# Head 15 of a differential-attention layer as a row-scale batch of its own, with four token blocks' output products taken into the attention and partial sums kept in DRAM

## The chip, the cores and the metric

The kernel runs on one core of a Trainium2 chip. The metric is the device time of one execution in microseconds (us). The engines are named as in the profile: PE (TensorE matmul), PEld (its weight loads), DVE (VectorE), ACT (ScalarE), POOL (GpSimd), SP (SyncE, which issues most of the DMAs; ACT issues the rest). A "q" behind an engine's name, as in ACTq, is its instruction queue.

## The reference

Two decoder layers on a 1024 x 1024 input, cut here to what the change touches (layer 1, differential attention):

```python
h = rmsnorm(x, pre_norm_g[1])
q, k, v, g = split(h @ w_in)              # 16 heads, two query/key maps of 64 each, v of 128
probs = softmax(logits + rel_bias)        # causal
attn = probs[:, :, 0] - lam * probs[:, :, 1]
out = attn @ v
out = rmsnorm(out, subln_g) * (1 - lambda_init)   # per token and head: the "row scale"
gated = silu(g) * out
x = x + rmsnorm(gated @ w_out, post_norm_g[1])
```

The row scale of a head is only known when the head's values are done. It multiplies the gated values before the output projection, so the products of a head's columns with w_out have to wait for it.

## The kernel before

Every fp32 product is three matmuls on a high and a low part of both operands: high times high, high times low, low times high (`out_mm`, L122 to L124). The high part is made by a cast on ACT, the low part by a subtraction on DVE or POOL (L92/L94 for the output weights, where even slots go to DVE and odd ones to POOL; L110/L111 for the gated values of eight 128x128 tiles; L476/L477 for those of four).

Layer 1 runs 16 heads of 8 query blocks in the order 6, 2, 3, 7, 4, 0, 1, 5. For each block there are logits (L760, L767), a softmax (DVE and ACT, L792 to L803), transposes of the probabilities into one PSUM bank (`attn_t`, L821, then a cast `ath` at L824 on ACT and a subtraction `atl` at L825 on DVE) and, for each pair of blocks, the products with v (`values`, L835 to L837). Behind a pair come the square (L843), its split (`sqh` L844, `sql` L845), `go` (L851) and `square_sum` (L857, L858), whose row `ssr` goes to DRAM as `ssd` (L860, L861).

`row_scales` (L863 to L876) makes the scales of a batch of heads: ACT issues the DMA `rss<-ssd` (L867), PE transposes the softmax sums into the same single bank that `attn_t` uses (L869), DVE copies them (L872) and works out a reciprocal root, and ACT issues `rsd<-rsr` (L876), from which the scales are read back, broadcast. Batches before are heads 0 to 7, 8 to 11 and 12 to 15. The first two are scaled inside the attention on POOL (`finish`). The gates of heads from LATE = 12 on are not multiplied in the attention: they go to DRAM (`sgd`, L642), and the output stage reads raw values, gates and scales for each token block and multiplies them (`gated`, L464 to L471).

The order of PE is written by the code. Between the steps of the attention a generator (`filler_gen`) puts projections of later heads, then the gates of heads 12 to 15, then the first output products (kt 0 to 11 of token blocks 0 and 1, where a kt is one 128-row slice of w_out and 16 of them make a sum). How much is pulled in after each step is set by `fill_total` from planned totals (`total`, `late`, RATE). The orders of DVE, ACT, POOL and, before, SP come from the scheduler.

The output stage (`output_stage`) does the first 512 output columns for all eight blocks, then the other 512. `first` takes the sum of a finished block's first half: a Square on ACT (L508) and a product on DVE (L509). In layer 1 the banks of PSUM for it are six, taken in rotation, beside the two of the filler. Each engine works through its queue in order, so one waiting instruction holds all that stand behind it.

## Time and profile before

| | |
|---|---|
| time, three runs (us) | 2181.16, 2179.63, 2179.52 |
| median (us) | 2179.63 |
| the profiled execution's own time (us) | 2180.56 |
| its span, first to last instruction (us) | 2178.6 |
| PE busy (us) | 2130.3 |
| DVE / ACT / POOL busy (us) | 1293.9 / 851.5 / 427.4 |
| mean granted TensorE clock | 0.994 |

The span is what the trace covers; the time has 1.96 us more around it. The profiled execution is 0.93 us above the median. A busy engine is one that executes an instruction; issuing a DMA doesn't count.

### The profile page before, as it was taken

Reading aid. Unit: us, or ns where it says so; the run is one execution under the profiler, and the core shown is the slowest. Engines: PE = TensorE matmul, PEld = TensorE weight load, DVE = VectorE, ACT = ScalarE, POOL = GpSimd, SP = SyncE. Lnnn points to the kernel's source line nnn. Section 1 sums busy time; section 2 is a strip of 40 time slices with the busy share of each in tenths; the row PEclk is TensorE's granted clock in tenths of the full one; section 3 lists DMA queues with packets and bytes.
Section 4 is the critical chain, followed back from the end, with each engine's and each line's share of the span. In section 5 each row is a group of like instructions: output and inputs, shape, how many; then the busy total and the mean of one; then the engine's idle time right before and its main releaser. Section 6 shows DMA issues by size and latency. Waiting matters only on the chain.

```text
span 2178.6 us, 31078 instructions
## 1 busy us (share of the span) xinstructions
PE 2130.3 (98%) x11861; PEld 1793.9 (82%) x11861; DVE 1293.9 (59%) x3188; ACT 851.5 (39%) x1638; POOL 427.4 (20%) x246
## 2 busy tenths in 40 slices
PE   7999999999999999999999999999999999999998
PEld 7888988898897788787888888888787878877876
DVE  6254344434437438736777667777777777776644
ACT  4121221122123333335555455554545555544321
POOL 2332501511512000121111111111133111211300
PEclk9999999999999999999999999999999999999999
DMA  4112112111212544311111111111244113334743
GB/s 164 65 39 68 57 39 73 47 54 54 63 55 98 176 158 166 121 49 42 40 46 42 40 49 42 39 37 43 85 136 134 47 38 95 115 101 146 256 152 133
DMA packets 98916, 185.48 MB, mean 85 GB/s; under 512 B 8848, under 2 KB 51024, under 8 KB 98640
## 3 DMA queue, kind: packets, MB, share of 16 engines
q1 hardware_dynamic: 63824, 166.50, 23.5%
q10 hardware_dynamic: 34944, 17.01, 2.6%
q8 instruction: 93, 1.52, 0.3%
q14 instruction: 55, 0.45, 0.1%
HBM read 147.67 MB, written 38.95 MB: 86 GB/s over the span
## 4 chain that ended last, share of the span: by engine, by line
PE 89%; DVE 4%; DMA 3%; issue 2%; ACT 1%; SPq 0%; POOL 0%; DVEq 0%; ACTq 0%; POOLq 0%
PE ps_mm L158 6%; PE ps_mm L157 6%; PE ps_mm L159 5%; PE ps_mm L215 5%; PE ps_mm L216 5%; PE ps_mm L217 5%; PE ps_mm L122 4%; PE ps_mm L123 4%; PE ps_mm L124 4%; PE ps_t L821 3%; PE ps_ret L398 3%; PE ps_s L760 3%; PE ps_mm L658 3%; PE ps_mm L167 3%; PE ps_mm L169 3%; PE ps_mm L168 3%
## 5 line engine op out<-in xcount | busy, mean ns | idle before, releaser
L83 POOL TENSOR_TENSOR w_l<-w_raw,w_h 128x1024 fp32r<-128x1024 f32 x112 | 271.6, 2431 | 1169.3 <-ACT w_h L82 1137.6
L797 ACT ACTIVATE e<-ps_s,nm 128x896 f32<-128x896 f32 (+7 forms) x256 | 189.8, 742 | 111.3 <-DVE nm L795 101.9
L215 PE MATMUL ps_mm<-RB,w_h 128*128 128x512 f32 x512 | 209.8, 410 | 0.4 <-ACT RB L150 0.4
L157 PE MATMUL ps_mm<-RA,w_h 128*128 128x512 f32 x512 | 204.6, 400 | 1.2 <-DVE sg L428 1.1
L158 PE MATMUL ps_mm<-RA,w_h 128*128 128x512 f32 x512 | 205.4, 401 | 0.0
L216 PE MATMUL ps_mm<-RB,w_h 128*128 128x512 f32 x512 | 202.9, 396 | 1.5 <-DVE RB L151 1.5
L217 PE MATMUL ps_mm<-RB,w_l 128*128 128x512 f32 x512 | 202.7, 396 | 0.0
L159 PE MATMUL ps_mm<-RA,w_l 128*128 128x512 f32 x512 | 202.4, 396 | 0.0
L824 ACT CAST ath<-ps_t 128x512 fp32r<-128x512 f32 (+1 forms) x192 | 91.9, 478 | 221.4 <-PE ps_t L821 205.5
L82 ACT CAST w_h<-w_raw 128x1024 fp32r<-128x1024 f32 x112 | 117.5, 1049 | 123.5 <-PE ps_mm L158 38.8
L792 DVE TENSOR_REDUCE mx<-ps_s 128x1 f32<-128x640 f32 (+2 forms) x192 | 119.4, 622 | 76.7 <-PE ps_s L767 72.5
L111 DVE TENSOR_TENSOR g_l<-w_raw,g_h 128x1024 fp32r<-128x1024 f32 x60 | 84.1, 1402 | 107.4 <-ACT g_h L110 107.3
L658 PE MATMUL ps_mm<-w_h,RB 128*128 128x256 f32 x512 | 147.3, 288 | 0.0
L169 PE MATMUL ps_mm<-w_h,RA 128*128 128x256 f32 x512 | 145.6, 285 | 0.0
L167 PE MATMUL ps_mm<-w_h,RA 128*128 128x256 f32 x512 | 144.9, 285 | 0.6 <-ACT RA L150 0.6
L168 PE MATMUL ps_mm<-w_l,RA 128*128 128x256 f32 x512 | 144.8, 284 | 0.1
L660 PE MATMUL ps_mm<-w_h,RB 128*128 128x256 f32 x512 | 143.5, 280 | 0.0
L659 PE MATMUL ps_mm<-w_l,RB 128*128 128x256 f32 x512 | 143.5, 280 | 0.0
L110 ACT CAST g_h<-w_raw 128x1024 fp32r<-128x1024 f32 x60 | 62.9, 1049 | 167.9 <-PE ps_mm L123 125.5
L157 PEld LDWEIGHTS ps_mm<-RA,w_h 128*128 128x128 f32 x512 | 96.4, 188 | 24.7 <-DVE sg L428 1.6
L217 PEld LDWEIGHTS ps_mm<-RB,w_l 128*128 128x128 f32 x512 | 96.5, 189 | 23.7
L159 PEld LDWEIGHTS ps_mm<-RA,w_l 128*128 128x128 f32 x512 | 96.6, 189 | 22.4
(216 smaller groups left out, 5408.4 us busy)
## 6 DMA issues: line engine op xcount, KB each, us to landing
w_raw<-in_wn SPq DMA_DIRECT2D x64, 512.0 KB
w_raw<-in_wv SPq DMA_DIRECT2D x32, 512.0 KB
w_raw<-in_wo SPq DMA_DIRECT2D x32, 512.0 KB
w_raw<-g SPq DMA_DIRECT2D x32, 512.0 KB
w_raw<-g1f SPq DMA_DIRECT2D x24, 512.0 KB
xt<-in_x SPq DMA_DIRECT2D x16, 512.0 KB
w_raw<-in_wg SPq DMA_DIRECT2D x16, 512.0 KB
g<-go ACTq DMA_DIRECT2D x32, 256.0 KB
```

The lines of the kernel that those rows point to most:

```text
L83: nc.gpsimd.tensor_sub(l, raw, _f32(h))
L157: nc.tensor.matmul(ps, wh[:, k], region[:, kt, cols], start=(kt == 0), stop=False)
L158: nc.tensor.matmul(ps, wh[:, k], region[:, 8 + kt, cols], start=False, stop=False)
L159: nc.tensor.matmul(ps, wl[:, k], region[:, kt, cols], start=False, stop=(kt == KT - 1))
L167: nc.tensor.matmul(ps, region[:, kt, cols], wh[:, k], start=(kt == 0), stop=False)
L168: nc.tensor.matmul(ps, region[:, kt, cols], wl[:, k], start=False, stop=False)
L169: nc.tensor.matmul(ps, region[:, 8 + kt, cols], wh[:, k], start=False, stop=(kt == KT - 1))
L215: nc.tensor.matmul(ps, wh[:, k], HR[:, kt, tok], start=(kt == 0), stop=False)
L216: nc.tensor.matmul(ps, wh[:, k], HR[:, 8 + kt, tok], start=False, stop=False)
L217: nc.tensor.matmul(ps, wl[:, k], HR[:, kt, tok], start=False, stop=(kt == KT - 1))
L658: nc.tensor.matmul(ps[:, t, :], HR[:, kt, cols], wh[:, k], start=(kt == 0), stop=False)
L797: nc.scalar.activation(e[:, 0:n], S[:, 0:n], AF.Exp, bias=nm, accum_out=(s0 if m == 0 else s1))
```

## The change

LATE goes from 12 to 15, so that the gates of heads 12 to 14 are made before their values and multiplied into `go`. The batches become 0 to 7, 8 to 11, 12 to 14 and 15. `row_scales` now comes ahead of `attn_t` in the code. The filler computes kt 0 to 11 for four token blocks instead of two: the sums of blocks 0 and 1 are copied by ACT and sent to DRAM (`part`), those of blocks 2 and 3 stay in PSUM. The filler's output products wait for the first weights of w_out (`wo_loaded`). The output stage's part for layer 1 is the new `last_heads`, in which SP's order is that of the code: products of blocks 4 to 7; then pairs of blocks, whose heads 12 to 14 are scaled on POOL, stored, split and multiplied (kt 12 to 14); then head 15 for all eight blocks in one 128x1024 tile (kt 15), after which DVE adds the partial sums to blocks 0 and 1. The first `gated8` of the second half is loaded ahead (`ahead`).

```diff
-LATE = 12
+LATE = 15
+AHEAD_TB = 4
-BATCHES = ((0, 8), (8, 12), (12, 16))
+BATCHES = ((0, 8), (8, 12), (12, 15), (15, 16))
...
+        def load_pair(t0):
+            raw = fp.tile([P, 2, 3, P], F32, tag="praw", name="praw", bufs=2)
+            rb = fp.tile([P, 2, 3, P], F32, tag="prb", name="prb")
+            for t in range(2):
+                nc.sync.dma_start(raw[:, t], self.g1r[2][t0 + t])
+            for t in range(2):
+                nc.sync.dma_start(rb[:, t], self.rsd[2][t0 + t:t0 + t + 1].broadcast_to([P, 3, P]))
+            nc.gpsimd.tensor_mul(raw, raw, rb)
+            return raw
+
+        def store_pair(t0, raw):
+            for t in range(2):
+                nc.sync.dma_start(self.gsrc(1, t0 + t, 12, 3), raw[:, t])
+
+        def split_pair(raw):
...
+            nc.scalar.copy(gh, raw)
+            low = nc.vector.tensor_sub(gl, raw, _f32(gh))
+            return (gh, gl), low
...
+        with self.tc.manual_schedule(engines={SP}):
+            for t in range(6, 8):
+                self.load_out(1, slots, 0, t)
...
+            for tb in range(AHEAD_TB, TB, 2):
+                two = (tb, tb + 1)
+                gs[tb] = ([self.gated8(1, ((t, 0, 8),)) for t in two], self.gated8(1, tuple((t, 8, 4) for t in two)))
+                head += early(tb, *gs[tb])
+                raws[tb - AHEAD_TB] = load_pair(tb - AHEAD_TB)
...
+                second_half(tb - AHEAD_TB)
+            accs = [bank() for tb in range(AHEAD_TB - 2)] + head
+            rb = None
+            for t0 in range(0, TB, 2):
+                store_pair(t0, raws[t0])
+                g, low = split_pair(raws[t0])
+                if t0 + 4 < TB:
+                    raws[t0 + 4] = load_pair(t0 + 4)
...
+                if t0 >= 2 and t0 + 2 < TB:
+                    second_half(TB - AHEAD_TB + t0 - 2)
+                for t in range(2):
+                    tb = t0 + t
+                    for _ in self.out_mm(accs[tb], g, slots[0], 12, 3, 3 * t, k_first=12 if tb < AHEAD_TB - 2 else 0):
+                        pass
+            with self.tc.issue_after(low.ins):
+                nc.vector.tensor_mul(raw, raw, rb)
+            gh = self.wp.tile([P, TB, P], F32R, tag="wh", name="g_h", bufs=3)
+            gl = self.wp.tile([P, TB, P], F32R, tag="wl", name="g_l", bufs=3)
+            nc.scalar.copy(gh, raw)
+            with self.tc.issue_after(low.ins):
+                nc.vector.tensor_sub(gl, raw, _f32(gh))
+            ahead = self.gated8(1, ((0, 0, 8),))
+            nc.sync.dma_start(self.g1f[1][:, :, 7, :].rearrange("t p q -> p t q"), raw)
+            for tb in range(TB):
+                for _ in self.out_mm(accs[tb], (gh, gl), slots[0], 15, 1, tb):
+                    pass
+                first(tb, accs[tb], parts[:, tb, :] if tb < AHEAD_TB - 2 else None)
+        return ahead
...
+                while not wo_loaded:
+                    yield None
...
+                            part = wk.tile([P, 512], F32, tag="sg", name="part", bufs=3)
+                            nc.scalar.copy(part, pss[t])
+                            nc.scalar.dma_start(self.part[t0 + t], part)
...
-            late = (DH - LATE) * 10.4 + 15.6
+            late = (DH - LATE) * 10.4 + 7.8 * AHEAD_TB
...
+                if rows is not None:
+                    row_scales(*rows)
                 fill_until(ready)
                 attn_t(h, i, A, 0)
                 t_done = clk["pe"]
                 if rows is not None:
-                    row_scales(*rows)
...
-                    if i == ORDER[-1] and h + 1 in (BATCHES[0][1], BATCHES[1][1]):
+                    if i == ORDER[-1] and h + 1 in (BATCHES[0][1], BATCHES[1][1], BATCHES[2][1]):
```

Below, an order's row is an instruction's line, operation, and names out<-in; rows of the changed kernel carry its own line numbers. The number behind a name (`ssd_89`) tells versions of one name apart.

PE where the scales of heads 8 to 11 are made, at the start of head 12, before (ident,e are the transposes of the probabilities, ident,s0all that of the softmax sums):

```order
L858 MATMUL ps_o<-sql,ones 128x256
L760 MATMUL ps_s<-RA 128x384 x2
L767 MATMUL ps_s<-RA 128x384 x2
L821 MATMUL ps_t<-ident,e 128x128 x4
L869 MATMUL ps_t<-ident,s0all 32x128
L658 MATMUL ps_mm<-w_h,RB 128x256
```

and in the changed kernel:

```order
L939 MATMUL ps_o<-sql,ones 128x256
L841 MATMUL ps_s<-RA 128x384 x2
L848 MATMUL ps_s<-RA 128x384 x2
L950 MATMUL ps_t<-ident,s0all 32x128
L902 MATMUL ps_t<-ident,e 128x128 x4
L725 MATMUL ps_mm<-w_h,RB 128x256
```

The transpose of the sums has moved ahead of the four of the probabilities; the rest of the place is as it was.

DVE at the border of heads 14 and 15 in the changed kernel, where the scales of heads 12 to 14 are now made (L95 is the subtraction for a slot of w_out, L926 `sql`, L941 `ssr`, L906 `atl`, L953 and on the scales):

```order
L95 TENSOR_TENSOR RA<-w_raw,RA 128x1024
L930 SCALAR_TENSOR_TENSOR go<-ps_o,subg,sg 128x256
L926 TENSOR_TENSOR sql<-sq,sqh 128x256
L941 COPY ssr<-ps_o 1x256
L873 TENSOR_REDUCE mx<-ps_s 128x1
L953 COPY rsr<-ps_t 24x128
...
L95 TENSOR_TENSOR RA<-w_raw,RA 128x1024
L876 TENSOR_SCALAR nm<-mx 128x1
L906 TENSOR_TENSOR atl<-ps_t,ath 128x4x128
L955 SCALAR_TENSOR_TENSOR rsv<-rss,rsv 24x128
L66 TENSOR_SCALAR rsr<-rsv 24x128
```

ACT at the same place in the changed kernel (L93 is the cast for a slot of w_out, L925 `sqh`, L905 `ath`, L878 the exponentials):

```order
L924 ACTIVATE sq<-ps_o 128x256
L93 CAST RA<-w_raw 128x1024
L925 CAST sqh<-sq 128x256
L937 DMA g1r_80<-go 128x2x128
L942 DMA ssd_89<-ssr 2x1x128
L93 CAST RA<-w_raw 128x1024
L878 ACTIVATE e,s0all<-ps_s,nm 128x384
L948 DMA rss<-ssd_89 24x128
L905 CAST ath<-ps_t 128x4x128
```

Before, no scales were made at this place. The loads of w_out that stood there still do, and the issue of `rss`, which needs what `ssd` stored, now stands ahead of a cast that the attention needs.

ACT where the first half of the output columns gives way to the second, before (L508 is the Square of `first`, L558 that of the second half):

```order
L476 CAST gh<-graw 128x512
L508 ACTIVATE junk,ssq<-ps_mm 128x512
L476 CAST gh<-graw 128x512
L508 ACTIVATE junk,ssq<-ps_mm 128x512 x3
L110 CAST g_h<-w_raw 128x1024 x2
L558 ACTIVATE yo,ssq<-ps_mm 128x512
```

and in the changed kernel (L576 casts a pair, L631 is head 15's cast, L503 the Square of `first`):

```order
L576 CAST pgh<-praw 128x768 x2
L93 CAST RA<-w_raw 128x1024 x2
L631 CAST g_h<-w_raw 128x1024
L111 CAST g_h<-w_raw 128x1024 x2
L503 ACTIVATE junk,ssq<-parts 128x512 x2
L503 ACTIVATE junk,ssq<-ps_mm 128x512 x5
L111 CAST g_h<-w_raw 128x1024
L503 ACTIVATE junk,ssq<-ps_mm 128x512
```

All eight Squares now stand behind the second of the two casts at L111. Its tile is the second half's kt 8 to 15 of block 0, which includes head 15.

## Rows read from the trace of the kernel before

**Rows 1.** The page's head: busy us, share of the span and instructions of each engine.
```profile
PE 2130.3 (98%) x11861; PEld 1793.9 (82%) x11861; DVE 1293.9 (59%) x3188; ACT 851.5 (39%) x1638; POOL 427.4 (20%) x246
```

**Rows 2.** PE's waits, 1920 to 1957: instruction, releaser, us, times, longest.
```profile
PE ps_o L836 <- DVE atl L825: 2.3, 1, 2.3
PE ps_t L821 <- DVE atl L825: 1.2, 1, 1.2
PE ps_s L760 <- ACT e L797: 0.9, 1, 0.9
```

**Rows 3.** PE's waits, 1975 to 2012 (one longer group left out).
```profile
PE ps_t L821 <- DVE atl L825: 2.0, 1, 2.0
...
PE ps_t L821 <- DVE nm L795: 0.5, 1, 0.5
```

**Rows 4.** Windows: busy us (and count) per engine, then granted clock, DMA share, GB/s.
```profile
1928.00:1932.00 4.00, 4.00 (x15) 3.32 (x14) 2.56 (x6) 2.62 (x5) 0.00 (x0) 0.60 0.72 271
1980.00:1984.00 4.00, 2.05 (x9) 1.75 (x9) 3.56 (x9) 1.48 (x4) 1.23 (x1) 0.80 0.38 125
1984.00:1988.00 4.00, 3.54 (x14) 2.43 (x13) 3.25 (x12) 1.34 (x5) 0.00 (x0) 0.78 0.44 126
2040.00:2060.00 20.00, 20.00 (x87) 16.08 (x87) 10.70 (x7) 6.30 (x7) 6.89 (x4) 1.00 0.87 299
```

**Rows 5.** Timeline where heads 8 to 11 get their scales: start, duration, instruction.
```profile
1751.40 0.69 DVE L825 TENSOR_TENSOR atl<-ps_t,ath 128x512 fp32r<-128x512 f32 x1
...
1752.14 0.28 PE L869 MATMUL ps_t<-ident,s0all 128*32 128x128 f32 x1 [1.40 <-DVE atl L825]
```

**Rows 6.** Timeline near 1924: POOL and DVE subtracting for w_out.
```profile
1923.13 2.40 POOL L94 TENSOR_TENSOR RA<-w_raw,RA 128x1024 fp32r<-128x1024 f32 x1 [27.09 <-PE ps_t L821]
...
1924.15 2.46 DVE L94 TENSOR_TENSOR RA<-w_raw,RA 128x1024 fp32r<-128x1024 f32 x1
```

**Rows 7.** Timeline near 1942: a 512 KB load of gated values, and its cast.
```profile
1941.51 0.33 SPq L106 DMA_DIRECT2D w_raw<-g1f  x1
1944.98 1.05 ACT L110 CAST g_h<-w_raw 128x1024 fp32r<-128x1024 f32 x1 [1.59 <-DMA w_raw<-g1f]
```

**Rows 8.** Timeline near 1979: a POOL subtraction, and DVE's `sql`.
```profile
1978.86 2.37 POOL L94 TENSOR_TENSOR RB<-w_raw,RB 128x1024 fp32r<-128x1024 f32 x1 [9.05 <-ACT RB L92]
1979.12 2.40 DVE L845 TENSOR_TENSOR sql<-sq,sqh 128x256 fp32r<-128x256 f32 x1
```

**Rows 9.** Timeline near 1750: the small transfers of the scales, little else moving.
```profile
1749.91 0.58 ACTq L861 DMA_DIRECT2D ssd<-ssr  x1
...
1751.53 0.33 ACTq L867 DMA_DIRECT2D rss<-ssd  x1
```

**Rows 10.** Timeline after the attention's end: the same chain among other loads.
```profile
2005.05 0.58 ACTq L861 DMA_DIRECT2D ssd<-ssr  x1
...
2010.01 0.35 ACTq L867 DMA_DIRECT2D rss<-ssd  x1
...
2013.94 1.08 DVE L874 SCALAR_TENSOR_TENSOR rsv<-rss,rsv 32x128 f32<-32x128 f32 x1 [8.42 <-DMA rss<-ssd]
...
2021.28 0.32 ACTq L876 DMA_DIRECT2D rsd<-rsr  x1
```

**Rows 11.** Groups by line, 2000 to 2180: count, busy us, mean ns, idle before.
```profile
L508 ACT ACTIVATE junk<-ps_mm 128x512 f32<-128x512 f32 x8 | 4.8, 594 | 4.4 <-PE ps_mm L124 4.3
L508 ACT ACTIVATION_READ_ACCUMULATOR junk<-ps_mm 128x1 f32 x8 | 1.5, 192 | 0.0
L509 DVE TENSOR_TENSOR yacc<-ps_mm,postg 128x512 f32<-128x512 f32 x8 | 5.5, 685 | 2.5 <-ACT junk L508 2.5
L94 DVE TENSOR_TENSOR RB<-w_raw,RB 128x1024 fp32r<-128x1024 f32 x2 | 2.4, 1216 | 0.0
L470 POOL TENSOR_TENSOR graw<-graw,rsb 128x512 f32<-128x512 f32 x8 | 12.3, 1543 | 28.3 <-DVE graw L469 18.5 <-DMA w_raw<-g1f 6.6 <-DMA g1f<-graw 2.1
```

**Rows 12.** PE's waits, 2000 to 2180.
```profile
PE ps_mm L124 <- DVE gl L477: 1.0, 1, 1.0
```

More of the change, by code (lines that the diff above doesn't have):

```diff
@@ L121, in out_mm @@
             k += g0
-            nc.tensor.matmul(ps, gh[:, k, :], wh, start=(kt == 0), stop=False)
+            nc.tensor.matmul(ps, gh[:, k, :], wh, start=(kt == k_first), stop=False)
             nc.tensor.matmul(ps, gh[:, k, :], wl, start=False, stop=False)
-            nc.tensor.matmul(ps, gl[:, k, :], wh, start=False, stop=(kt == NE - 1))
+            nc.tensor.matmul(ps, gl[:, k, :], wh, start=False, stop=(kt == k_last))
             yield 0.65
@@ L482, in product @@
                     if kq % 2 == 0:
-                        for _ in self.out_mm(ps, self.gated8(layer, ((tb, kq * 4, 8),)), slots[hf], kq * 4, 8):
+                        g = ahead if layer == 1 and tb + kq == 0 else self.gated8(layer, ((tb, kq * 4, 8),))
+                        for _ in self.out_mm(ps, g, slots[hf], kq * 4, 8):
                             pass
@@ L496, in second_half, with first @@
                     self.load_out(layer, slots, 1, t, fp.tile([P, D], F32, tag="x", name="w_raw", bufs=2))
-            def first(tb, ps):
+            def first(tb, ps, part=None):
                 if not acc:
@@ L506, in first @@
                         nc.sync.dma_start(acc["preg"], io["pre_g"][1:2, :].broadcast_to([P, D]))
+                if part is not None:
+                    nc.vector.tensor_add(part, ps, part)
+                    ps = part
                 junk = fp.tile([P, D], F32, tag="x", name="junk", bufs=2)
@@ L520, in output_stage @@
             else:
-                for t in range(6, 8):
-                    self.load_out(1, slots, 0, t)
-                for tb in range(2, TB, 2):
-                    two = (tb, tb + 1)
-                    g = [self.gated8(1, ((t, 0, 8),)) for t in two]
-                    head += [bank() for t in two]
-                    for t in two:
-                        for _ in self.out_mm(head[t], g[t - tb], slots[0], 0, 8):
-                            pass
-                    g8 = self.gated8(1, tuple((t, 8, 4) for t in two))
-                    for t in two:
-                        for _ in self.out_mm(head[t], g8, slots[0], 8, 4, 4 * (t - tb)):
-                            pass
-                    second_half(tb - 2)
-                second_half(TB - 2)
-                for tb in range(TB):
-                    product(head[tb], 0, tb, 3)
-                    first(tb, head[tb])
+                ahead = self.last_heads(fp, slots, head, bank, first, second_half)
                 lead = TB
@@ L685, in filler_gen @@
                     self.load_out(1, slots, 0, t)
+                while not wo_loaded:
+                    yield None
                 g = self.gated8(1, ((0, 8, 4), (1, 8, 4)))
[L687 to L692 removed]
+                for t0 in range(0, AHEAD_TB, 2):
+                    last = 11 if t0 + 2 < AHEAD_TB else NE - 1
+                    pss, nxt = [], []
+                    for t in range(2):
+                        pss.append(pmm.tile([P, 512], F32, tag="mm", name="ps_mm", bufs=2))
+                        yield from self.out_mm(pss[t], early[t0 + t], slots[0], 0, 8, k_last=last)
+                        if last == 11:
+                            early.append(self.gated8(1, ((t0 + 2 + t, 0, 8),)))
+                    for t in range(2):
+                        yield from self.out_mm(pss[t], g, slots[0], 8, 4, 4 * t, k_last=last)
+                        if last == 11:
+                            part = wk.tile([P, 512], F32, tag="sg", name="part", bufs=3)
+                            nc.scalar.copy(part, pss[t])
+                            nc.scalar.dma_start(self.part[t0 + t], part)
+                        else:
+                            heads.append(pss[t])
+                    if last == 11:
+                        g = self.gated8(1, ((t0 + 2, 8, 4), (t0 + 3, 8, 4)))
             filler = filler_gen()
@@ L914, in attention_layer @@
                 if rows is not None:
-                    row_scales(*rows)
-                    todo += [None] * 8 + [(tb, h0) for h0 in range(*BATCHES[rows[0]], 4) for tb in range(TB)] + [()]
+                    if rows[0] < 2:
+                        todo += [None] * 8 + [(tb, h0) for h0 in range(*BATCHES[rows[0]], 4) for tb in range(TB)] + [()]
                     rows = None
@@ L976, in run @@
         self.g1f = [self.dr.tile([TB, P, 8, P], F32, name="g1f%d" % k) for k in range(2)]
+        self.part = self.dr.tile([AHEAD_TB - 2, P, 512], F32, name="part")
         self.x1d = self.dr.tile([T, D], F32, name="x1d")
```

56 lines of the change are left out of this document (36 added, 20 removed).

## The prediction

> **What bounds the kernel now.** The page's first part comes first: PE is busy for 2130.3 us of a span of 2178.6 [rows 1]. So 48.3 us, 2.2%, is idle, and a change that does the same matmuls can win only from idle time or from a clock that is not full. The matmuls are 11862 before and 11863 after by the two orders, so what PE does costs nothing new; what counts is where it stands still. Next come PE's waits by stretch, for they name who ended each stop, and the windows, for the granted clock falls after some stops. At the border of heads 14 and 15 PE waits 2.3, 1.2 and 0.9 us [rows 2], all on DVE or ACT work of the softmax that came late. Inside head 15 it waits 2.0 and 0.5 [rows 3]. The clock after the longer stops shows only part of full speed for some 4 to 8 us: 0.60 in one window, 0.80 and 0.78 in two others, against 1.00 in a quiet stretch [rows 4]. Each such dip costs 4 x 0.40 = 1.6 or 4 x (0.20 + 0.22) = 1.7 us. In the output stage PE is full: 87 matmuls in 20 us, 0.23 each and 0.69 for a kt [rows 4].
>
> **The change part by part.** The sum is made against the profiled execution's 2180.56 us, which is 0.93 above the median of the three runs shown; it is carried over to the median at the end.
>
> *Filler.* 24 kts (72 matmuls) leave the output stage for the attention: 24 x 0.69 = 16.6 us off the one and onto the other. The sum is zero. So is the gate work moved earlier: the products are the same.
>
> *(a) Scales ahead of the transposes.* At heads 8 and 12, the transpose of the sums waits 1.40 us for `atl` to empty the one bank that `attn_t` has just filled [rows 5]. After the change it finds the bank empty, and the four transposes behind it wait instead for a copy of 32 or 64 rows on DVE. I take 0.6 for that (the copy and its way). Two places: 2 x (1.4 - 0.6) = -1.6. If the copy is held up as `atl` was, 0; if the wait vanishes, -2.8.
>
> *(b) The border of heads 14 and 15.* Removed are the three waits, 2.3 + 1.2 + 0.9, and the 1.6 of clock behind the first: -6.0. The first was a subtraction for w_out on DVE that took 2.46 us in place of 1.2 while POOL did one of its own from 1.02 us earlier, so `atl` stood behind it [rows 6, 11]. The second and third came behind a load of gated values that needed 3.1 us from the end of its issue to the cast [rows 7] and then held ACT and DVE.
>
> But the same loads of w_out still stand here, and now the scales of heads 12 to 14 do too. No filler lies between the last values of head 14 and their `square_sum`, since the filler waits for w_out. Behind each other come: `ssr` behind a DVE subtraction that POOL can hold up, 1.0 (0 to 1.3); `sqh` behind a w_out cast and `sql` behind a w_out subtraction, 3.0 (1.0 with nothing held up, 4.0 with all of it: 2.46 + 1.05 + 0.4); the bank, 0.5; ACT's issue of `rss`, which waits for `ssd` to land and holds back `ath`, 1.2 (between the quiet 1.6 and the 4.9 of the busy stretch, less the filler of about 2.8 that can stand before `ath` is wanted [rows 9, 10]); DVE's wait for `rss` ahead of the next `atl`, 1.3 (0 to the 3.9 from issue to use [rows 10]). Together 7.0, and one clock dip, 1.7. With -6.0 that is +2.7. The ends are -5.5 (only the bank) and +8.
>
> A rule of the Trainium skill speaks against this place. First the rows: `sql` began 0.26 us after a POOL subtraction and took 2.40 in place of some 0.4, ending 0.29 after POOL's end [rows 8], and the one of 2.46 ended 1.08 after POOL's end [rows 6]. The page "SBUF — State Buffer" (section "Who interferes with whom") says that a DVE instruction with two SBUF inputs and a GpSimd one that reads SBUF share a port that one of them locks, so that the second waits for the whole rest of the first. The traced pairs agree. By that rule each of the subtractions that I count as held up here, in block 6 and in pair 4 below could pay a whole POOL instruction, 2.4 us, 7.2 together where I take 4.0, and the sum would be 3.2 us higher.
>
> *(c) Inside head 15.* The 2.0 us wait and its dip of 1.7 came from that `sql`; with the smaller one of 0.5 that is -4.2. In the changed order a gated subtraction and one for w_out stand ahead of one `atl`: +1.0 (0 to 2.4). Net -3.2.
>
> *(d) End of the attention.* The same steps in the same order, with one gated cast and subtraction (1.05 + 1.2) more ahead of an `atl`, of which 1.7 lie beside filler: +0.5 (0 to 2.3).
>
> *(e) The output stage.* The 1.0 us that PE waited for a late `gl` goes [rows 12]: the scaling of heads 12 to 14 is now off the end. Three waits may come.
>
> First, block 6's gated values: their casts stand on ACT behind the issue of `rsd`, which waits for DVE's root. The root ends about 13.6 us after the attention's end (`rss` 9.5 after it [rows 10], then 1.1 and eleven steps of 0.28), then two w_out casts (2.1) and the cast (1.05) and a subtraction that POOL may hold up (1.2 to 2.4): 18.0 to 19.2, where PE has 24 kts, 16.6 us, and the wait before. I take +1.1 (0 to 2.6).
>
> Second, pair 4: two w_out casts and two subtractions stand ahead of its split, which can be caught by a POOL subtraction of 2.4: +1.9 (0 to 3.8).
>
> Third, and most certain, the first bank of the second half. The banks go round, and the next is block 4's. Before, five blocks of work lay between that bank's last matmul and its next use. Now it is three kts, 2.1 us. In between ACT must do five Squares of 0.79 and DVE two additions and five products of 0.69, one subtraction of 1.2 among them [rows 11]: 0.7 + 7 x 0.69 + 1.2 = 6.7 us from the first kt 15, against the 8 x 0.69 = 5.5 that PE works there: +1.2 at least, 1.1 if the first addition begins a little earlier. All the Squares also stand behind a cast of gated values that include head 15, so behind a store to DRAM and a load back. At 3.1 each [rows 7] and a cast of 1.05, the cast ends 7.3 us after head 15's multiplication, five Squares take 3.9 more and a product 0.7: 11.9. PE ends kt 15 at 7.8 if it waited for head 15 (1.05 + 1.2 + 5.5), later by up to 3.2 if it still had a pair to do: 0.9 to 4.1. I take 2.6, the middle, and a clock dip of 1.7.
>
> Sum of (e): -1.0 + 1.1 + 1.9 + 2.6 + 1.7 = +6.3.
>
> **Sum**: -1.6 + 2.7 - 3.2 + 0.5 + 6.3 = +4.7. From 2180.56 that is 2185.3; at the median, 2184.3.
>
> **The rivals.** *A smooth border* (the other side, faster). The small transfers land as in the quiet row (1.6 us) and POOL's subtractions start after DVE's. Then the border pays 0.5 + 1.3 and no dip, (d) is 0, block 6 and pair 4 are ready and the first bank costs its floor of 1.1: -1.6 - 4.2 - 3.2 + 0.1 = -8.9, 2170.7. For it: loads for the whole border are few, and 1.6 is measured. Against it: at the end of the attention, with w_out being loaded, the same DMA took 4.9. It decides as soon as PE's waits at the border stay under 2 us.
>
> *No change that can be told.* The border is as forecast, but the reload of head 15 is in time, so the first bank costs 1.1 and no dip: 3.2 less, +1.5, 2181.1. For it: 11.9 against 7.8 to 11.0 is the softest pair of numbers here.
>
> *The fixed SP order slips.* A pair needs a load (3.9 as `rss`), POOL's multiplication (768 columns, between the 1.54 for 512 [rows 11] and 2.40 for 1024 [rows 6]: 2.0), a cast of 0.8, a subtraction of 1.0: 7.7 to 8 us, where PE uses a pair up in 6 x 0.69 = 4.1. If pairs 4 and 6 are not loaded well ahead, each costs 3.8: +12.3, 2191.9. For it: each store, load and buffer stands in one queue, and a late one holds the rest. Against it: pair 0 can be split right at the attention's end, so its buffer is free early.
>
> **How the numbers follow.** The forecast gets 0.34, no change 0.26, the smooth border 0.24, the slipping order 0.16. A measurement of this kernel can tell about 0.2%, 4.4 us, from no change; the bounds are 2175.3 and 2184.0. The forecast's own range, 2181 to 2188, lies across the upper one: 0.11 under it, 0.23 over. Faster is the smooth border and 0.02 of the no-change case: 0.26. Same: 0.24 + 0.11 = 0.35. Slower: 0.23 + 0.16 = 0.39. The range reaches from 2169, which leaves out less than half of the smooth border's spread, to 2193, which takes in the centre of the slipping order.
>
> **What would show it.** (a): at heads 8 and 12 the 1.40 us wait of the sums' transpose is gone, and the first transpose of the probabilities waits about 0.6. (b): between head 14's last values and the third filler stretch of head 15, PE's waits add up to 7, with DVE subtractions of over 2 us beside POOL's, and one clock window well under 1. (e): PE's first matmul of the second half waits for a product of `first` (`yacc`), and the cast before the Squares waits for a load of g1f. The forecast is wrong if PE's waits from 1900 on add up to less than before, or if a pair's `pgl` ends a wait of over 3 us.

## The result, and the profile after

The changed kernel is slower: 2200.59 us (four executions, 2197.42 to 2205.99) against 2179.57, a ratio of 1.010 with a 95% interval of 1.0087 to 1.0113. That is 21 us, where 4.7 were forecast, and above the stated range. The profiled execution took 2197.42 and is the fastest of the four; its span is 2195.5, 16.9 longer than before.

The page's head shows one matmul more in PE than before [rows 1], and more time in which it does nothing, 62.1 us against 48.3:

```profile
PE 2133.4 (97%) x11862; PEld 1794.5 (82%) x11862; DVE 1299.2 (59%) x3196; ACT 853.5 (39%) x1637; POOL 422.3 (19%) x242
```

PE's waits of the changed kernel from 1880 to 2100, which answer to [rows 2, 3, 12]:

```profile
PE ps_mm L123 <- ACT pgh L576: 6.1, 1, 6.1
PE ps_o L938 <- ACT sqh L925: 4.0, 1, 4.0
PE ps_t L902 <- DVE e L884: 3.3, 2, 1.7
PE ps_t L902 <- DVE nm L876: 3.1, 1, 3.1
PE ps_o L939 <- DVE sql L926: 1.8, 1, 1.8
PE ps_s L841 <- ACT e L878: 1.7, 1, 1.7
PE ps_mm L125 <- DVE pgl L577: 1.3, 1, 1.3
```

One of these has the place of a wait of before: the 3.1 us one stands at the same transposes of head 15 as the 2.0 of [rows 3], with ten transposes of probabilities still to come in both kernels. At the others PE did not wait before. To say where the time went, the span is cut at two instructions that both kernels have: the first sum of squares of layer 1 (the first matmul on `sqh`) and the last transpose of the softmax sums, which is the end of the attention.

| us | before | changed | difference | without the 24 kts (16.6) |
|---|---|---|---|---|
| to the first sum of squares | 994.8 | 991.9 | -2.9 | |
| from there to the last transpose of sums | 1009.6 | 1037.3 | +27.7 | +11.1 |
| from there to the span's end | 174.2 | 166.3 | -7.9 | +8.7 |

The first row is code that the change doesn't touch. Before, two stretches of 3.4 us at half clock stood there (at 709 and 917); the changed kernel's profiled execution has neither. The loss is 11.1 in the attention and 8.7 in the output stage, so without those 2.9 the span would have been 19.8 longer and not 16.9. Of the 11.1, 7.5 are idle time of PE, 1.7 the clock (in which only the time counts in which PE worked at half), and 1.9 more busy time than the 24 kts explain.

**The border of heads 14 and 15.** The timeline of the changed kernel there:

```profile
1959.57 1.04 ACT L93 CAST RA<-w_raw 128x1024 fp32r<-128x1024 f32 x1 [1.84 <-DMA w_raw<-in_wo]
1960.52 0.40 ACT L925 CAST sqh<-sq 128x256 fp32r<-128x256 f32 x1
1960.69 2.34 POOL L95 TENSOR_TENSOR RA<-w_raw,RA 128x1024 fp32r<-128x1024 f32 x1 [6.02 <-ACT RA L93]
1960.95 2.36 DVE L926 TENSOR_TENSOR sql<-sq,sqh 128x256 fp32r<-128x256 f32 x1 [1.27 <-ACT sqh L925]
1960.97 0.58 PE L938 MATMUL ps_o<-sqh,ones 128*128 128x256 f32 x1 [4.02 <-ACT sqh L925]
1963.37 0.58 PE L939 MATMUL ps_o<-sql,ones 128*128 128x256 f32 x1 [1.82 <-DVE sql L926]
```

The square was done at 1957.7. `sqh` stood behind a w_out cast that waited 1.84 us for its load, and `sql` began 0.26 us after a POOL subtraction and ended with it. PE stood still for 4.02 and 1.82 us with one short matmul between, and then for 0.37 and 1.66. What the clock did is in the windows of the same place:

```profile
1956.00:1960.00 4.00, 0.95 (x9) 0.81 (x7) 3.31 (x6) 2.16 (x5) 0.00 (x0) 0.90 0.51 179
1960.00:1964.00 4.00, 1.21 (x3) 0.92 (x4) 2.37 (x2) 0.92 (x2) 2.34 (x1) 0.50 0.63 164
1964.00:1968.00 4.00, 3.63 (x12) 2.37 (x12) 3.06 (x11) 2.44 (x5) 0.00 (x0) 0.50 0.47 138
```

The granted clock is at 1.2 GHz, half, for 10.2 us from 1959.2 on, where each dip before lasted 3.4 [rows 4]. PE stood still in part of these 10.2 us, and there the clock costs nothing: it was busy for 6.3 of them, so the dip cost some 3.2 us.

**The output stage.** SP's and ACT's timelines, then POOL's, of the changed kernel:

```profile
2035.56 12.50 SPq L107 DMA_DIRECT2D w_raw<-g1f  x4
2048.11 0.90 SPq L562 DMA_DIRECT2D praw<-g1r  x2
...
2052.12 2.31 SPq L570 DMA_DIRECT2D g1f<-praw  x2
2060.99 0.80 SPq L562 DMA_DIRECT2D praw<-g1r  x2
...
2062.78 0.90 SPq L570 DMA_DIRECT2D g1f<-praw  x2
2067.83 0.80 SPq L562 DMA_DIRECT2D praw<-g1r  x2
...
2069.64 0.91 SPq L92 DMA_DIRECT2D w_raw<-in_wo  x2
```

```profile
2039.55 0.84 ACT L576 CAST pgh<-praw 128x768 fp32r<-128x768 f32 x1 [11.08 <-POOL praw L565]
...
2076.83 1.04 ACT L93 CAST RA<-w_raw 128x1024 fp32r<-128x1024 f32 x1 [15.81 <-DMA w_raw<-in_wo]
...
2079.06 1.56 ACT L576 CAST pgh<-praw 128x768 fp32r<-128x768 f32 x2
```

```profile
2066.93 1.84 POOL L565 TENSOR_TENSOR praw<-praw,prb 128x768 f32<-128x768 f32 x1 [3.44 <-DMA prb<-rsd]
```

Read it from the end. PE waited 6.06 us (from 2073.9) for the third pair's cast at 2079.06. That pair had been scaled by 2068.8, so its cast could have run then; it stood on ACT behind two w_out casts. Their loads were issued at 2069.64, behind the fourth pair's load (2067.83), which needed the second pair's buffer, free only when its store (2062.78) had landed. The third pair's load (2060.99) had waited in the same way for the first pair's store. That one was issued at 2052.12, though the pair was ready at 2039.5: SP had been held by four loads of gated values from 2035.6 to 2048.

### The profile page after: what moved, and what is told of

The parts are those of the page before. It is cut to its first block, busy times and chain, and to the rows that moved or that the text cites. A ratio compares the mean times of both kernels' runs of the same rounds, so it can differ in the third digit from the quotient of the medians.

```text
span 2195.5 us, 31049 instructions
## 1 busy us (share of the span) xinstructions
PE 2133.4 (97%) x11862; PEld 1794.5 (82%) x11862; DVE 1299.2 (59%) x3196; ACT 853.5 (39%) x1637; POOL 422.3 (19%) x242
## 4 chain that ended last, share of the span: by engine, by line
PE 89%; DVE 5%; DMA 2%; issue 2%; ACT 2%; SPq 1%; POOL 0%; ACTq 0%; DVEq 0%; POOLq 0%
PE ps_mm L159 5%; PE ps_mm L158 5%; PE ps_mm L160 5%; PE ps_mm L216 5%; PE ps_mm L217 5%; PE ps_mm L218 5%; PE ps_mm L123 5%; PE ps_mm L125 4%; PE ps_mm L124 4%; PE ps_t L902 3%; PE ps_ret L399 3%; PE ps_s L841 3%; PE ps_mm L168 3%; PE ps_mm L170 3%; PE ps_mm L169 3%; PE ps_mm L725 3%
## 5 line engine op out<-in xcount | busy, mean ns | idle before, releaser
L878 ACT ACTIVATE e<-ps_s,nm 128x896 f32<-128x896 f32 (+7 forms) x256 | 190.1, 743 | 115.3 <-DVE nm L876 107.4
L905 ACT CAST ath<-ps_t 128x512 fp32r<-128x512 f32 (+1 forms) x192 | 92.1, 480 | 214.2 <-PE ps_t L902 193.4
L111 ACT CAST g_h<-w_raw 128x1024 fp32r<-128x1024 f32 x60 | 62.9, 1050 | 171.6 <-PE ps_mm L124 121.7
L902 PE MATMUL ps_t<-ident,e 128*128 128x128 f32 x576 | 100.3, 283 | 14.5 <-DVE e L884 8.0
```

The source lines that it names most:

```text
L878: nc.scalar.activation(e[:, 0:n], S[:, 0:n], AF.Exp, bias=nm, accum_out=(s0 if m == 0 else s1))
```

## The experiments

The kernels, with the stretches of the table above from their own traces. "Stretch" is from the first sum of squares to the last transpose of sums, "tail" from there to the span's end. Each ratio is against executions of the kernel before taken beside it (medians 2178.61 to 2179.57). "From head 12" is the part of the stretch from head 12's first sum of squares on. It leaves out attention that the change hardly touches, where dips of 3.4 us come and go: one at 1639 stands in the executions of e3, e5, e8, e11 and e12 and in no other.

| kernel | median us | ratio, 95% interval | stretch | from head 12 | tail |
|---|---|---|---|---|---|
| before | 2179.57 | 1 | 1009.6 | 224.7 | 174.2 |
| changed | 2200.59 | 1.0087 to 1.0113 | 1037.3 | 252.6 | 166.3 |
| e1_border | 2198.79 | 1.0083 to 1.0110 | 1036.3 | 252.1 | 169.0 |
| e2_spfree | 2188.53 | 1.0032 to 1.0057 | 1035.8 | 252.2 | 155.3 |
| e3_casts | 2202.55 | 1.0093 to 1.0121 | 1037.2 | 251.5 | 167.4 |
| e4_dve | 2195.24 | 1.0065 to 1.0093 | 1033.1 | 249.5 | 163.4 |
| e5_store | 2198.19 | 1.0074 to 1.0102 | 1037.8 | 252.4 | 165.5 |
| e6_hold | 2199.25 | 1.0078 to 1.0105 | 1032.2 | 248.5 | 169.9 |
| e7_all | 2185.16 | 1.0017 to 1.0038 | 1033.3 | 249.6 | 155.3 |
| e8_rows | 2179.31 | 0.9989 to 1.0007 | 1009.8 | 224.1 | 174.8 |
| e9_noborder | 2204.14 | 1.0102 to 1.0133 | 1029.1 | 245.6 | 174.1 |
| e10_batch | 2181.79 | 1.0003 to 1.0022 | 1012.3 | 227.4 | 173.9 |
| e11_best | 2174.60 | 0.9972 to 0.9989 | 1006.7 | 221.7 | 173.3 |
| e12_freedve | 2188.01 | 1.0025 to 1.0050 | 1033.1 | 247.7 | 155.2 |

**e1_border**

```diff
-                    nc.scalar.copy(sqh, sq)
-                    nc.vector.tensor_sub(sql, sq, _f32(sqh))
+                    mark["sqh"] = nc.scalar.copy(sqh, sq)
+                    mark["sql"] = nc.vector.tensor_sub(sql, sq, _f32(sqh))
...
-                    for t in range(4):
-                        self.load_out(1, slots, 0, t)
+                    self.load_out(1, slots, 0, 0)
+                    with self.tc.issue_after(mark["sqh"].ins), self.tc.issue_after(mark["sql"].ins):
+                        for t in range(1, 4):
+                            self.load_out(1, slots, 0, t)
```

> The changed kernel with one place swapped in ACT's queue: at the border of heads 14 and 15, the cast sqh goes ahead of the cast for the second of the four w_out slots. Theory (queue order at the border): the 4.02 us that PE waits for sqh falls to about 1.3, sql is no longer caught by POOL (1.82 to about 0.5), and the 10.2 us of half clock behind it become 3.4: some 3 + 1 + 3.4 = 7 us faster than the changed kernel, about 2193. Rival (PE is late there for the loads of w_out themselves, whatever the order): the wait moves to the next instruction that needs a slot of w_out, and the time stays near 2200.

On ACT `sqh` now stands ahead of the w_out cast. PE's waits of this kernel from 1930 to 2100, two of the groups:

```profile
PE ps_mm L123 <- ACT pgh L576: 8.1, 1, 8.1
PE ps_o L938 <- DVE go L930: 2.9, 1, 2.9
```

The wait fell from 4.0 to 2.9, where about 1.3 was expected, and `sql` was no longer caught. Its releaser is now `go` on DVE, which stood behind a w_out subtraction (L95) and must read the bank first: the cast on ACT was 1.1 of the 4.0, and DVE's queue bounded the rest. From head 12 on only 0.4 is won: 1.7 came back at a transpose behind `atl` a little later. And the third pair's wait grew from 6.1 to 8.1. The median is 1.8 below the changed kernel's, with ranges that overlap, so no gain is shown. This one place in ACT's queue is at most a small part of the loss.

**e2_spfree**

```diff
-        with self.tc.manual_schedule(engines={SP}):
+        with ExitStack():
```

> The changed kernel without SP's fixed order in the output stage; the scheduler orders SP. Theory (the fixed order slips, because a store that waits holds the next pair's load): PE's wait for the third pair's cast, 6.06 us, changes by more than 2 us either way, and the store of the first pair is issued within 5 us of its scaling. Rival (ACT's order alone, a w_out cast that waits for its load ahead of the pair's cast): the wait stays within 2 us of 6 as long as those casts stand ahead of it.

PE's longest waits of this kernel from 1930 to 2100:

```profile
PE ps_o L938 <- ACT sqh L925: 3.7, 1, 3.7
PE ps_t L902 <- DVE nm L876: 2.7, 1, 2.7
PE ps_o L939 <- DVE sql L926: 1.8, 1, 1.8
```

No pair stands among them any more. The first pair's store is issued at 2044.96, 3.7 us after its scaling ended, and the w_out loads go one by one between the pairs, the first two at 2047.6 and 2050.8. The tail is 155.3, 11.0 shorter than the changed kernel's and 2.3 shorter than before's less the filler (174.2 - 16.6 = 157.6). The time is 12 us less, and the attention is as it was. The rival's condition held and its forecast failed: two w_out casts still stood on ACT ahead of the third pair's, and PE didn't wait there, since their loads had been issued at 2062.4 and 2066.3 and not at 2069.6. The loss in the output stage is that of the fixed SP order.

**e3_casts**

```diff
-                if t0 >= 2 and t0 + 2 < TB:
-                    second_half(TB - AHEAD_TB + t0 - 2)
+                if t0 >= 4:
+                    second_half(t0)
```

> The changed kernel with the last four loads of the second half's w_out slots issued one pair later, so that on ACT two casts stand behind the third pair's cast and not ahead of it. Theory (ACT's order): the third pair was scaled by 2068.8 and its cast waited for a w_out load until 2079; PE's wait of 6.06 + 1.30 us falls to under 1.5 and the 6.8 us of half clock go: 8 to 10 us faster than the changed kernel, about 2191, less what the later w_out slots cost at the second half's start (0 to 5). Rival (the pair itself is late): the wait stays over 4 us.

The third pair's cast ran at 2070.0, in time. The same two w_out casts then held the fourth pair's: ACT's timeline of this kernel:

```profile
2081.20 1.04 ACT L93 CAST RA<-w_raw 128x1024 fp32r<-128x1024 f32 x1 [10.33 <-DMA w_raw<-in_wo]
...
2083.42 0.83 ACT L576 CAST pgh<-praw 128x768 fp32r<-128x768 f32 x1
```

PE waited 6.8 us there, and nothing was gained. The cast that waits moved one pair on with its loads, so neither expectation held as written: ACT's queue is where the stop becomes one of PE's, and SP's is where it starts.

**e4_dve**

```diff
-        eng = nc.vector if (t % 2 == 0) else nc.gpsimd
+        eng = nc.vector if (t % 2 == 0 or layer == 1) else nc.gpsimd
```

> The changed kernel with all low parts of layer 1's w_out made on DVE, none on POOL. Theory (POOL's subtractions hold DVE's): no DVE subtraction of 256 or 512 columns takes over 1 us in head 15; the 1.82 us wait for sql at the border becomes less than 0.7, and the kernel is 2 to 5 us faster than the changed one. Rival (DVE's own load): eight more subtractions of 1.22 us stand in DVE's queue and PE's waits for atl and for the softmax at the border grow by as much as they save: within 2 us of 2200, or slower.

`sql` took 0.42 us on the mean of six from 1940 to 2030, where it had been 0.99. The wait for it is gone. The first one at the border is 4.4 where it was 4.0, and ends with `go` on DVE, behind a w_out subtraction. The stretch is 4.2 shorter (3.0 of it from head 12 on), the tail 2.9, the time 5.3. The theory's numbers hold, a little exceeded; DVE's longer queue cost less than POOL's hold.

**e5_store**

```diff
+                if tb > AHEAD_TB:
+                    store_pair(0, raws[0])
                 raws[tb - AHEAD_TB] = load_pair(tb - AHEAD_TB)
...
+                if t0 > 0:
+                    store_pair(t0, raws[t0])
```

> The changed kernel, SP's order fixed as there, with one step moved: the first pair's store is issued ahead of the second pair's load and not five transfers later. Theory (the third pair's load waits for the buffer that the first pair's store still reads, and all later w_out loads wait behind it on SP): the store is issued about 4 us and the third pair's load about 5 us earlier, PE's wait for the third pair's cast falls from 6.06 to 1 to 2.5 us, and the kernel is 4 to 7 us faster than the changed one, about 2195. Rival (bandwidth: the transfers take that long in any order): the wait stays over 4.5 us.

SP's timeline of this kernel, the third pair's load, the second pair's store and the fourth pair's load:

```profile
2054.99 2.15 SPq L562 DMA_DIRECT2D praw<-g1r  x2
2060.66 0.79 SPq L564 DMA_DIRECT2D prb<-rsd  x2
2061.50 0.91 SPq L570 DMA_DIRECT2D g1f<-praw  x2
2067.33 0.80 SPq L562 DMA_DIRECT2D praw<-g1r  x2
```

The third pair's load came 6 us earlier, where 5 were expected. But its scales wait for a single buffer, the second pair's store follows only behind them, and the fourth pair's load still waits for that store to land (5.8 us). So the w_out loads were issued at 2070.4, as late as before the edit. PE's wait is 4.4, between the two expectations, though just under the rival's 4.5. The median is 2.4 less, the span of the profiled execution 0.3 more, so no gain is shown. One store moved doesn't mend a queue in which each pair waits for the store of the pair two before it.

**e6_hold**

```diff
+HOLD = 3.3
...
             def pull():
+                if clk["fill"] >= clk["cap"]:
+                    return False
...
             clk["pe"] = clk["fill"] = 0.0
+            clk["cap"] = total + 10.4 - HOLD
...
+                        if h + 1 == BATCHES[2][1]:
+                            clk["cap"] = 1e9
                         fill_until(ready_o)
```

> The changed kernel with 24 matmuls of head 15's gate (5.6 us) held back from the steps before the border of heads 14 and 15 and issued around it: 12 between head 14's last values and their sum of squares, 6 before the logits, 6 before and behind the next transposes. Theory (the border is left without filler, so PE waits out the chain square, split, sum): of PE's 7.9 us of waits at the border under 2.5 are left and the 10.2 us of half clock fall to 3.4 or none; 1.5 to 3 us of new waits stand in the steps that gave up their filler; 5 to 8 us faster than the changed kernel, about 2194. Rival (the waits only move to where the filler was taken): the waits from 1880 to 1990 add up to the same within 2 us, and the gain is under 2.

The border's waits are gone, and others of the same size stand where the filler was taken. PE's waits of this kernel, 1930 to 2100, two of them:

```profile
PE ps_mm L124 <- ACT pgh L577: 8.6, 1, 8.6
PE ps_t L905 <- DVE atl L909: 4.3, 2, 3.0
```

From 1880 to 1990 PE's waits add up to 12.5 against 11.4 in the changed kernel, and the median is 1.3 less: both as the rival said. The stretch is 5.1 shorter, but 1.1 of that lies ahead of head 12. From the second sum of squares of head 14 to the first of head 15 it is 0.5 shorter with six matmuls (1.4 us) fewer, so nothing is won there; the rest of head 15 is 3.5 shorter with six more, since the 3.1 us wait is 0.8 there and no dip follows it. Then the output stage took it back: the third pair came no earlier, PE came sooner, and waited 8.6 where it had waited 6.1; half clock lasted 13.7 us there in place of 6.8. As long as the pairs' chain ends last, what is won in the attention is waited out there.

**e7_all**: the edits of e2_spfree, e4_dve and e6_hold together.

> The changed kernel with three edits together: SP's order in the output stage left to the scheduler, the low parts of layer 1's w_out all on DVE, and the filler held back for the border. Theory (the losses are SP's order 10 to 12, POOL's hold 4 to 5, the empty border 5 to 8, and add up): 2176 to 2182, level with the kernel before or a little faster. Rival (they share one loss, the late w_out loads): no better than the 2188.5 of the scheduler's SP order alone.

2185.16, 15.4 less than the changed kernel, where the theory wanted 2176 to 2182: about SP's order (12) and POOL's hold (5.3), and not what filler was to add. It stays 0.17 to 0.38% above before.

**e12_freedve**: e2_spfree and e4_dve without the held filler.

> The changed kernel with SP's order left to the scheduler and the low parts of layer 1's w_out on DVE, no filler held back. Theory (the two losses are apart): the 10 to 12 us of SP's order and the 4 to 5 of POOL's hold add up, 2183 to 2185, and holding filler back gave nothing on top. Rival (holding filler back gave 3 or more of the 2185.2 of the three edits together): 2187 or more.

In the traces holding filler back gives nothing once POOL is out of the way: stretch and tail are those of e7_all within 0.2, and from head 12 on this kernel is 1.9 shorter (e7_all has no dip at 1639, which makes up for it). By the medians it is 2.9 above e7_all, over the rival's 2187; the two ranges overlap (2183.3 to 2189.3 and 2182.1 to 2188.5), and its profiled execution took 2183.3. This is not settled by these runs.

**e8_rows**

```diff
+                if rows is not None:
+                    row_scales(*rows)
                 fill_until(ready)
                 attn_t(h, i, A, 0)
                 t_done = clk["pe"]
                 if rows is not None:
-                    row_scales(*rows)
```

> The kernel before with one part of the change: the scales' transpose ahead of the transposes of the probabilities. Theory: at heads 8 and 12 the wait of 1.40 us goes and one of about 0.4 comes, 1.0 at each and 2.0 together; too little to be told from no change (2176.6 to 2179.6). Rival (what stands behind the transposes is late now): no gain in the time from one sum of squares to the next around heads 8 and 12.

At heads 8 and 12 the wait is 0.4 in place of 1.4. From one sum of squares to the next 0.1 and 0.9 were won, 1.0 in all and not 2.0: at head 8 the next transposes waited longer. In the time it can't be seen.

**e9_noborder**

```diff
-BATCHES = ((0, 8), (8, 12), (12, 15), (15, 16))
+BATCHES = ((0, 8), (8, 12), (12, 16))
...
-            row_scales(3)
+            row_scales(2)
...
```

> The changed kernel without scales at the border: heads 12 to 15 are one batch again, scaled behind head 15, everything else (gates early, four blocks ahead, the output stage's order) as changed. PE's order differs only in head 14's last sum of squares, behind filler now, and the transpose of the sums. The time says little, since the pairs' scales come later and the output stage waits for them; what tells is the stretch from the first sum of squares of layer 1 to the last transpose of the sums, 1037.3 us in the changed kernel and 1009.6 before, of which 16.6 is filler that moved. Theory (the border's chain stands there with no filler): the stretch falls to 1028 or less and no clock dip stands at the border. Rival (the gates and w_out loads moved to this place are the loss): 1034 or more.

The windows of this kernel at the border, to be held against those of the changed one above:

```profile
1956.00:1960.00 4.00, 4.00 (x29) 3.42 (x28) 3.85 (x8) 2.38 (x5) 1.05 (x1) 1.00 0.40 136
1960.00:1964.00 4.00, 3.85 (x21) 2.96 (x20) 3.91 (x9) 2.21 (x4) 3.71 (x2) 1.00 0.64 179
```

PE is busy throughout and the clock is full, with the w_out loads still at this place. The stretch is 1029.1, 8.2 less than in the changed kernel; the theory wanted 1028 or less, which was missed by 1.1, the rival 1034 or more. Of the 8.2, 1.3 lie ahead of head 12, where PE's work is the same in both. From head 12 on it is 6.9: 4.4 from the second sum of squares of head 14 to the first of head 15, with the same number of matmuls, and 2.5 behind that. Dips of 3.4 us are left at 1945 and 1969, so what went around the border is waiting and not half clock. The edit also puts head 14's last sum of squares behind filler; it doesn't tell that from the scales.

**e10_batch**

```diff
-BATCHES = ((0, 8), (8, 12), (12, 16))
+BATCHES = ((0, 8), (8, 12), (12, 15), (15, 16))
...
-                    nc.sync.dma_start(raw, self.g1r[2][tb])
+                    nc.sync.dma_start(raw[:, 0:3], self.g1r[2][tb])
+                    nc.sync.dma_start(raw[:, 3:4], self.g1r[3][tb])
...
```

> The kernel before with the new batches alone: heads 12 to 14 get their scales at the border, head 15 at the end, the output stage reads both for each block; gates, filler and SP's order as before. Here 12 matmuls of filler stand between head 14's last values and the sum of squares. Theory (the scales cost only where filler is missing): the stretch from the first sum of squares to the last transpose of the sums is within 3 us of the 1009.6 before. Rival (the chain of the scales costs whatever stands beside it): 1014 or more.

The stretch is 1012.3, 2.7 above before's. PE's two longest waits of this kernel at the border, 1938 to 1956:

```profile
PE ps_t L871 <- DVE atl L827: 1.6, 1, 1.6
PE ps_t L823 <- DVE atl L827: 1.2, 1, 1.2
```

With filler between the last values and the sum of squares, the same scales cost 2.7 us at the same place in the program, where taking them out of the changed kernel gave 4.4 to 6.9. The stretch is within the theory's 3 us. But this kernel also has its late gates as filler in heads 12 to 15, and in e6_hold filler moved to the border only moved the waits. So the place is cheaper in a kernel with more filler; that 12 matmuls beside the scales are enough is not shown.

**e11_best**: the edits of e8_rows and e4_dve on the kernel before.

> The kernel before with two small edits: the scales' transpose ahead of the transposes of the probabilities, and the low parts of layer 1's w_out all on DVE. Theory (POOL's subtractions hold DVE's at 1924 and 1979): the waits of 2.3 and 1.95 us and their two clock dips of 1.7 go, about 1.5 comes back in DVE's longer queue, 2.0 come from the transpose: 5 to 8 us faster than before, 2172 to 2175. Rival (DVE's queue becomes the late one): within 2 us of before.

2174.60 us, 0.11 to 0.28% under before, and the fastest kernel of this study. Its windows where the dips of before began [rows 4]:

```profile
1926.00:1930.00 4.00, 4.00 (x21) 2.96 (x19) 2.44 (x5) 3.60 (x7) 0.00 (x0) 1.00 0.39 132
1980.00:1984.00 4.00, 3.30 (x16) 2.79 (x17) 2.31 (x10) 1.30 (x5) 0.00 (x0) 1.00 0.42 137
```

POOL does nothing there, PE stops for less and the clock stays full. The gain is 5.0 by the medians, the lower end of what was expected. Against e8_rows, which has the other of the two edits, it is 4.7, so nearly all of it is POOL's subtractions.

## Why the prediction was wrong

Its sign was right, its size was not: +4.7 forecast, +16.9 in the profiled execution's span and +21 in the medians. Four steps failed: it took the early gates to cost nothing, it took a wait inside head 15 to go that stayed, it priced the border's clock by one short dip, and it held the pairs' buffers to be free early under SP's fixed order. By its own terms:

| term | forecast | measured |
|---|---|---|
| (a) scales ahead of the transposes | -1.6 | -1.0 |
| (b) border of heads 14 and 15 | +2.7 | +5.1 |
| (c) inside head 15 | -3.2 | +0.6 |
| (d) end of the attention | +0.5 | 0 |
| (e) output stage | +6.3 | +8.7 |
| gates earlier, heads 12 to 14 | 0 | +4.6 |

**(a)** was right in kind: the 1.40 us wait [rows 5] gave way to one of 0.37, and from one sum of squares to the next the two places won 0.3 and 0.7. The changed kernel's timeline at head 12:

```profile
1747.75 0.29 PE L950 MATMUL ps_t<-ident,s0all 128*32 128x128 f32 x1
...
1748.41 0.66 PE L902 MATMUL ps_t<-ident,e 128*128 128x128 f32 x4 [0.37 <-DVE rsr L953]
```

**(b)** had the right place, and a sum of waits that came near by luck: 4.02 + 1.82 + 0.37 + 1.66 = 7.9 against 7.0. `sqh` and `sql` took 5.8 where 3.0 was the term and 4.0 its end; the bank took 0.4 of its 0.5; and for `ssr` and the two waits for `rss`, 3.5 together, there is one of 1.66 at later logits. The clock was mis-sized: one dip of 1.7, priced from the stops of about 2 us before, where 10.2 us at half clock, 6.3 of them with PE busy, cost 3.2. 7.9 + 3.2 - 6.0 = +5.1. e9_noborder (4.4 less around the border and 6.9 from head 12 on) shows that the border's scales, with the sum of squares that they ask for there, cost this; in e10_batch, a kernel with more filler in these heads, they cost 2.7.

**(c)** is the term with the wrong sign. The 2.0 us wait and its dip were to go. They stand at the same transposes as before and have grown: 3.1 us from 2003.8 on, with a dip of 3.4. A w_out cast that waited 4.5 us for its load held ACT ahead of the square, `sqh` and `ath`, and `sql` took 1.9 beside POOL's subtraction. The step that failed is that the changed order would take w_out's cast and subtraction away from that square; they still stand beside it. In e4_dve, where POOL does no such subtraction, the wait at this place is 1.3.

**(e)** came out near in size by luck, for the wrong reasons. What I called "third, and most certain", the second half's first bank, didn't happen. PE's and DVE's timelines where the second half begins (the last kt 15 ends at 2097.5):

```profile
2097.48 0.40 PE L123 MATMUL ps_mm<-RB,g_h 128*128 128x512 f32 x1
2097.52 0.68 DVE L504 TENSOR_TENSOR yacc<-parts,postg 128x512 f32<-128x512 f32 x1
...
2098.19 0.69 DVE L504 TENSOR_TENSOR yacc<-ps_mm,postg 128x512 f32<-128x512 f32 x1
```

The first matmul follows without a wait, before DVE has read the banks of blocks 2 to 7. So its bank can only be one that was empty by then, and those of blocks 0 and 1 were, their sums having been added into SBUF at 2092.8 to 2094.2. That the banks go round to block 4's was read from the code and not from a row. The other half of the sign came true and cost nothing: the cast ahead of the Squares waited 4.8 us for a load of g1f (2095.29), and nothing that PE needed hung on the Squares.

What PE lost stands at pair 4, the third pair, where +1.9 (0 to 3.8) was forecast for two w_out casts ahead of its split. The casts were there; that they would wait for their loads was not in the term. Block 6 cost nothing. The reason is that of the rival that got 0.16, "the fixed SP order slips": 6.06 + 1.30 of waits, and 6.8 us at half clock with PE busy in 4.3 of them, 2.1, together 9.5 where 12.3 - 4.7 = 7.6 was its price; less the 1.0 that went [rows 12], 8.5 against the 8.7 of the tail. The sentence against it, that pair 0 "can be split right at the attention's end, so its buffer is free early", is what failed: it was split at 2042, but its buffer was free only when a store had landed that SP issued ten microseconds later. e2_spfree confirms the rival as a whole: the same work with another SP order has none of these waits.

**Heads 12 to 14** were taken as costing nothing ("So is the gate work moved earlier"). The products are the same, but the gates' weights now load at other points of the attention. PE waits there for 0.6 (at 1806), 0.7 (1862), 1.5 and 1.7 us, 4.6 together, where it had waited at none of these places. The changed kernel's timeline near 1893:

```profile
1890.65 4.73 POOL L84 TENSOR_TENSOR w_l<-w_raw,w_h 128x1024 fp32r<-128x1024 f32 x2 [5.87 <-ACT w_h L83]
1891.47 1.60 DVE L882 SCALAR_TENSOR_TENSOR arr<-arr,neglam,s0all 128x1 f32<-128x1 f32 x1
1893.33 2.61 DVE L884 SCALAR_TENSOR_TENSOR e<-e,arr 128x512 f32<-128x512 f32 x1
...
1896.08 0.63 PE L902 MATMUL ps_t<-ident,e 128*128 128x128 f32 x4 [1.53 <-DVE e L884]
```

Two POOL subtractions stood beside the softmax, each DVE step ended just behind one of them, and PE waited 1.5; a second wait of 1.7 at 1922 has no POOL work beside it, only DVE's queue. That these waits come from the earlier gates is argued, not shown; the two longer ones are there in all the kernels with early gates (e1 to e7, e9 and e12) and in none of the others.

The sum of the attention's terms is 9.3 and the stretch lost 11.1; 0.7 of the rest lies in heads 8 to 11, which are unchanged, and about 1 is open. Open too is why the changed kernel's four executions lie 8.6 us apart (2197.4 to 2206.0); those of before lay 2.6 apart in the first comparison, but 8.5 in a later one of 18. The changed kernel's profiled execution is its fastest, and that of before is 1.0 above its median, so some 4 us of the 21 are in no trace here.

The rule of the Trainium skill that was weighed, from the page "SBUF — State Buffer" (section "Who interferes with whom"), bears up: the second of a DVE instruction with two SBUF inputs and a GpSimd one that reads SBUF waits for the whole rest of the first. `sql` ended with POOL's subtraction at 1963.3 and not some 0.4 after its start; and size doesn't matter, as DVE's and POOL's timelines of the changed kernel show in the output stage:

```profile
2037.61 1.91 POOL L565 TENSOR_TENSOR praw<-praw,prb 128x768 f32<-128x768 f32 x1 [31.89 <-DVE rss L74]
2037.84 1.82 DVE L73 TENSOR_TENSOR rss<-rsr 8x128 f32<-8x128 f32 x1
```

A product of 8 x 128 elements that otherwise takes 0.28 us took 1.82, until POOL's had ended. The sum by that rule would have been 3.2 us higher, which is nearer, and e4_dve's 5.3 and most of e11_best's 5.0 are what taking POOL out was worth.

## What to carry to other kernels

A hand-written order on a DMA queue must be walked with the landing of every store that a later load's buffer waits for, not with its issue: here one late store passed through two more pairs and a weight load to a cast on ACT, and PE paid 6 us. Work that has a long chain of small steps on several engines (a scale, a sum) costs more where less is queued for the matmul engine; before it is put at a new place, look at what filler stands there, 2.7 us against 4.4 to 6.9 in this case, and whether it can be had without a wait where it is taken (e6_hold). Price the clock by the stops that the change makes, not by those that it removes, and count of a dip only the time in which the engine works. And before a wait is booked as gone, find its instruction in the new order and look at what stands beside it there.

## What the runs showed of the hardware

Two stops of 4.02 and 1.82 us, 0.6 apart, came with 10.2 us at 1.2 GHz, from inside the first stop on, three times as long as with the single stops of about 2 us before; with the 6.1 us stop in the output stage it was 6.8 us, and with the 8.1 and 8.6 us stops of e1_border and e6_hold 13.7. The longest stop alone doesn't set the length: in e10_batch five stops of 0.5 to 1.6 us within 10 us came with 10.2 us, and the changed kernel's single stop of 3.1 us with 3.4. A small DVE instruction next to a POOL one waited as long as a large one, 1.8 us for 8 x 128 elements.
